# A hybrid decoder layer in float32: gate part moved to the output projection, pinned block products, six open merges

## The chip, the cores and the metric

The kernel runs on one core of one Trainium2 chip. The metric is the device time of one execution in microseconds. The kernel before took 2693.59 us, the median of three runs (2691.98 to 2694.18). All matrix products run on TensorE (PE in the profile); VectorE (DVE) and ScalarE (ACT) prepare operands and take results out of PSUM; GpSimd (POOL) builds some small sums and issues some transfers; SyncE (SP) issues most of the DMA transfers, strictly one after the other.

## The reference, cut to what matters

One layer over 512 tokens of width 2048, one batch. A condition vector `c` gives a shift, a scale and a gate for each channel.

```python
u = RMSNorm(x) * (1 + scale(c)) + shift(c)
# one projection of u (w_in) gives q, k, v of three mixers, their z and the merge gates g
A: differential attention, 8 heads: (softmax(q1 k1) - lam * softmax(q2 k2)) @ v, RMS norm
B: retention, 8 heads, q and k rotated in pairs, decay matrix instead of softmax, RMS norm
C: dilated sliding windows, 3 groups x 8 heads
y_b = (mixer_b(u) * silu(z_b)) @ P_b            # 1024 -> 2048, for b in A, B, C
m   = sum_b sigmoid(g_b) * y_b
x   = x + gate(c) * (m @ W_out)
out = RMSNorm(x) * w
```

The gate is `gate(c) = silu(c) @ w_ada[:, 4096:6144] + b_ada[4096:6144]`, a vector of 2048 channels from a matrix of 2048 x 2048 float32, 16 MB. The rotation pairs channel 2i with 2i+1: `x * cos + swap(x) * sin`, where the swap exchanges the two and changes a sign. All values are float32; the kernel reaches that accuracy by splitting each operand in a high part `h` (rounded to the matmul type) and a low part `l = x - h`, and by three matmuls for each product: h·h, h·l and l·h (`mm3`).

## The kernel before, in words

Channels lie on partitions, 128 at a time, and the 512 tokens along the free dimension. The normalised input is `uh`, `ul` (16 blocks of 128 channels). The program has nine stages in time:

1. Start and forms (0 to 243 us): norms, shift and scale, and the token sides `fh`, `fl` of the block products.
2. Block products (243 to 968): the values of the three mixers and the merge gates of A and B, each a unit of 1024 columns by a scheme of seven products of half-size blocks. A unit is a list of jobs; a job has a preparation (load a raw block `xr`; for the sums, four in-place adds at L583; the cast `xh` on ScalarE, L552 or L584; the low part `xl` on VectorE, L553 or L585) and a multiplication. When a list ends, a closing (`keep`, `p2_done`, `sum_done` at L604 to L614) takes the products out of PSUM and hands the result on: values are stored by GpSimd, gates go through a sigmoid first.
3. C heads (968 to 1665): projections of one head after another, scores, softmax, values. Beside them GpSimd builds one bias a head for the merge gates of C (L674 to L687): four loads of weights, products with the shift, and sums into a tile `br`; TensorE adds its rows up (L691) and VectorE stores the column.
4. Merge of C (1665 to 1760), a call of `gate_phase`: 16 output blocks `db`. Each is a product of eight weight blocks (`w_half`: load of 512 KB, cast at L147, low part at L148) with `yh`, `yl`, the mixer's result in eight row blocks; then VectorE multiplies by the gate column `gsg`, adds the partial sum `gpr` of the earlier mixers, and stores it to `part`, from where the next merge reads it.
5. A heads (1760 to 2090). 6. Merge of A (2090 to 2175).
7. B (2175 to 2410): four pairs of heads, each with two rotations (L1102 to L1106), the splits of `q` and `k` (L1136 to L1146), scores and values. 8. Merge of B (2410 to 2510), whose closing gives the merged operand `mh`, `ml` instead of a partial sum.
9. Output projection (2510 to 2692): five groups of output columns (512, 512, 512, 256, 256). For each step of a group a tile of `w_out` is loaded, cast (L1223), split (L1224) and multiplied with four token blocks; then `residual` multiplies by `gate`, adds `x` (`hx`) and collects squares; the final norm follows.

In a merge, the last row blocks of `y` are not ready when it begins. So `y_start` opens three products with the first six of the eight row blocks, between which leftover work of the mixer stands (`left`), and each product is closed in turn with the last two row blocks. Within the merges of C and A stands the gate part (L768, called by `gate_aux` after each close): 32 pieces of 512 KB of `w_ada` (`gwa`) are loaded on SP, each folded by two VectorE operations into `gacc`; after eight pieces a sum over partitions by two matmuls (`gate_sum`) is added to a row (`grow`) that is stored to DRAM and later loaded, spread over 128 partitions, as `gate` (L1215).

The order on each engine is the order in which a scheduler places the recorded instructions, by its own estimate of when they become ready; a queue runs them strictly in that order, and an instruction that waits holds back those behind it. PSUM has eight banks: two tagged `pj`, six tagged `at`. Weight tiles have three buffers, the raw blocks of the block products three and their split parts two, `gsg` two, `gpr` one, `br` one.

## Time and profile before

| | |
|---|---|
| median of three runs | 2693.59 us |
| time of the profiled execution | 2694.27 us |
| its span from first to last instruction | 2692.5 us |
| mean granted TensorE clock | 0.986 of full |
| TensorE busy | 2578.1 us, 96% |
| VectorE busy | 1695.3 us, 63% |
| ScalarE busy | 1034.6 us, 38% |
| GpSimd busy | 268.9 us, 10% |
| DMA | 448 MB, 166 GB/s on average |

A row of instructions names the line of the program, the engine, the operation, the tile written and the tiles read, their shape, how many there were, the busy time, the mean duration of one in ns, and the engine's idle time in front of them with what ended it. A row of waits gives the line that waited, who released it, the total, the number of waits and the longest. Durations of single matmuls overlap, since TensorE is pipelined; their start-to-start distance is what counts.

### The profile page before, as it was taken

The numbers are of one execution on the slowest core, as the hardware profiler recorded it, in microseconds if no ns is written. First come the engines' busy times: TensorE is split into PE (matmuls) and PEld (weight loads), VectorE is DVE, ScalarE is ACT, GpSimd is POOL, SyncE is SP. The second block draws the span as 40 slices with busy tenths as digits, with TensorE's granted clock in tenths as the row PEclk, the third lists the DMA queues.
The fourth block names the chain that finished last, engine by engine and source line by source line (L and its number), as shares of the span: only waits on it lengthen the run. The fifth ranks groups of instructions, "written<-read, shape, count | busy, mean of one in ns | idle before, by whom it ended". The sixth has DMA issues, their size and how long they took to land.

```text
span 2692.5 us, 33258 instructions
## 1 busy us (share of the span) xinstructions
PE 2578.1 (96%) x13091; PEld 2188.5 (81%) x13091; DVE 1695.3 (63%) x2456; ACT 1034.6 (38%) x1388; POOL 268.9 (10%) x271
## 2 busy tenths in 40 slices
PE   6899999999999999899999999999999899998998
PEld 5677878789999988788888888788887677777888
DVE  7995887877787744334443444657766667776434
ACT  4234433333343433333333333246665134443222
POOL 3432000000000022132211220000000000000000
PEclk9999999999999999999999999999999899999999
DMA  9776666666656655334444444943232773325632
GB/s 347 247 275 239 231 212 219 219 220 209 212 196 204 208 145 137 94 106 126 113 118 108 112 125 128 286 126 87 86 94 84 231 236 90 106 82 176 219 102 102
DMA packets 413420, 448.17 MB, mean 166 GB/s; under 512 B 24696, under 2 KB 308042, under 8 KB 412112
## 3 DMA queue, kind: packets, MB, share of 16 engines
q1 hardware_dynamic: 383784, 395.61, 46.6%
q0 software_dynamic: 9760, 33.59, 4.0%
q10 hardware_dynamic: 19720, 16.86, 1.8%
q8 instruction: 102, 1.67, 0.3%
q14 instruction: 54, 0.44, 0.1%
HBM read 405.56 MB, written 40.44 MB: 166 GB/s over the span
## 4 chain that ended last, share of the span: by engine, by line
PE 78%; DVE 12%; DMA 5%; ACT 2%; issue 2%; POOL 0%; SPq 0%; DVEq 0%; ACTq 0%; POOLq 0%
PE pj L154 15%; PE pj L153 15%; PE pj L152 15%; PE at L154 10%; PE at L153 10%; PE at L152 10%; DVE acc L312 3%; DMA xr<-in_w_in_dram 2%; DVE xl L553 1%; DMA part<-gsg 1%; DVE rt L1105 1%; DVE rs L995 1%; DMA gpr<-part 1%; DVE wl L148 1%; ACT xh L552 1%
## 5 line engine op out<-in xcount | busy, mean ns | idle before, releaser
L154 PE MATMUL pj<-uh,wl 128*128 128x512 f32 x1552 | 610.2, 393 | 12.1 <-DVE wl L148 9.5
L152 PE MATMUL pj<-uh,wh 128*128 128x512 f32 x1552 | 614.1, 396 | 4.8 <-ACT wh L147 4.8
L153 PE MATMUL pj<-ul,wh 128*128 128x512 f32 x1552 | 608.5, 392 | 0.0
L148 DVE TENSOR_TENSOR wl<-wr,wh 128x1024 fp32r<-128x1024 f32 x226 | 282.4, 1251 | 368.0 <-ACT wh L147 349.2
L147 ACT CAST wh<-wr 128x1024 fp32r<-128x1024 f32 x228 | 239.0, 1050 | 540.3 <-PE pj L153 395.3
L154 PEld LDWEIGHTS pj<-uh,wl 128*128 128x128 f32 x1552 | 293.8, 189 | 76.3 <-DVE wl L148 11.9
L152 PEld LDWEIGHTS pj<-uh,wh 128*128 128x128 f32 x1552 | 294.1, 189 | 63.9 <-ACT wh L147 5.0
L153 PEld LDWEIGHTS pj<-ul,wh 128*128 128x128 f32 x1552 | 294.0, 189 | 58.6
L584 ACT CAST xh<-xr 128x2048 fp32r<-128x2048 f32 x72 | 137.6, 1912 | 235.8 <-PE at L154 104.1
L583 DVE TENSOR_TENSOR xr<-xr 128x512 f32<-128x512 f32 x288 | 197.3, 690 | 41.5 <-DMA xr<-in_w_in_dram 36.0
L585 DVE TENSOR_TENSOR xl<-xr,xh 128x2048 fp32r<-128x2048 f32 x72 | 164.7, 2289 | 43.3 <-ACT xh L584 43.1
L152 PE MATMUL at<-yh,wh 128*128 128x512 f32 x384 | 155.2, 405 | 18.4 <-ACT yh L218 11.8
L553 DVE TENSOR_TENSOR xl<-xr,xh 128x2048 fp32r<-128x2048 f32 x54 | 123.8, 2293 | 55.3 <-ACT xh L552 54.8
L154 PE MATMUL at<-yh,wl 128*128 128x512 f32 x384 | 154.5, 402 | 3.9 <-DVE wl L148 3.7
L153 PE MATMUL at<-yl,wh 128*128 128x512 f32 x384 | 153.9, 401 | 0.0
L552 ACT CAST xh<-xr 128x2048 fp32r<-128x2048 f32 x54 | 103.0, 1908 | 128.0 <-PE at L153 52.0
L152 PE MATMUL at<-fh,xh 128*128 128x256 f32 x384 | 108.7, 283 | 0.0
L153 PE MATMUL at<-fl,xh 128*128 128x256 f32 x384 | 108.7, 283 | 0.0
L154 PE MATMUL at<-fh,xl 128*128 128x256 f32 x384 | 108.7, 283 | 0.0
L152 PEld LDWEIGHTS at<-yh,wh 128*128 128x128 f32 x384 | 74.8, 195 | 36.0 <-ACT yh L218 13.0
L153 PE MATMUL at<-xl,fh 128*128 128x512 f32 x240 | 93.5, 390 | 1.1 <-DVE xl L553 1.1
L154 PE MATMUL at<-xh,fl 128*128 128x512 f32 x240 | 93.4, 389 | 0.0
(408 smaller groups left out, 5144.9 us busy)
## 6 DMA issues: line engine op xcount, KB each, us to landing
wr<-in_w_in_dram SPq DMA_DIRECT2D x196, 512.0 KB, 3.9
xr<-in_w_in_dram SPq DMA_DIRECT2D x144, 512.0 KB, 4.4
xr<-in_w_in_dram SPq DMA_DIRECT2D x54, 1024.0 KB, 5.6
wa<-in_w_ada_dram SPq DMA_DIRECT2D x20, 1024.0 KB, 9.8
gwa<-in_w_ada_dram SPq DMA_DIRECT2D x32, 512.0 KB, 5.7
wr<-in_w_out_dram SPq DMA_DIRECT2D x32, 512.0 KB, 3.8
wr<-in_w_in_dram SPq DMA_DIRECT2D x32, 448.0 KB, 6.7
wb<-in_w_ada_dram SPq DMA_DIRECT2D x12, 1024.0 KB, 8.8
```

The costliest lines, as they stand in the source:

```text
L147: act.copy(h, r)
L148: low.tensor_sub(l, r, h.bitcast(F32))
L152: nc.tensor.matmul(ps, lhsT=ah, rhs=bh, start=start, stop=False)
L153: nc.tensor.matmul(ps, lhsT=ah, rhs=bl, start=False, stop=False)
L154: nc.tensor.matmul(ps, lhsT=al, rhs=bh, start=False, stop=stop)
L312: dve.scalar_tensor_tensor(out=acc, in0=wa[:, j, :], scalar=sc[:, k:k + 1], in1=acc, op0=ALU.mult, op1=ALU.add)
L552: act.copy(h, r)
L553: dve.tensor_sub(l, r, h.bitcast(F32))
L583: dve.tensor_add(r[:, o, :], r[:, o, :], r[:, a, :])
L584: act.copy(h, r)
L585: dve.tensor_sub(l, r, h.bitcast(F32))
L995: dve.reciprocal(rs, rs)
```

## The change

Six edits in one:

- **Block products.** The order of their matmuls, casts, splits, sums and sigmoids on the engines is pinned to the order in which they are written (`keep_in_program_order`), and the loop over the jobs is written as three steps: the raw block of two jobs ahead is loaded, the next job's block is summed and split, the present job is multiplied. A unit's closing is cut in three (`done_z`, `done_s`, `done_rest`), one behind each of three following jobs; a gate's sigmoid comes one job later still.
- **Biases.** `br` has two buffers, a load starts in each head and its sum is taken in the next, and the doubled load stands at head 4 instead of head 1.
- **Merges.** In C and A six products are opened with seven of the eight row blocks, in B four with six; one tile (`late`) holds the last row blocks' weights for all of them. The first two products use the `pj` banks. From then on each further product is a whole one, and a close follows each (two in B, while more than one is behind).
- **Gate part.** It moves from the merges of C and A to the output projection: two pieces after each step of the first column group, one after each later step, with two buffers for `gwa`. `gate` is loaded as the bias `b_ada`, spread over the partitions, and the sums are added to it in place; the row `grow` and its way through DRAM are gone.
- **Rotation.** The four VectorE products of 32 rows that read the swapped rows become four ScalarE copies and one VectorE product of 128 rows; the table `sin` is loaded swapped, in four pieces. The second copy of a low part of `k` is made by ScalarE.
- **B's end.** The values of the last pair's first head move into the last projection.

```diff
+    def pin(instr):
+        if pinned[0]:
+            tc.keep_in_program_order(instr)
...
     for i, (_, mul, done) in enumerate(jobs):
-        nxt = jobs[i + 1][0]() if i + 1 < len(jobs) else None
-        if i < HJ:
-            form_build(i)
+        sums = form_build(i) if i < HJ else None
+        due, deferred[:] = list(deferred), []
+        if i + 2 < len(jobs):
+            raws.append(jobs[i + 2][0]())
+        nxt = x_split(raws.pop(0)) if raws else None
+        if sums:
+            form_split(*sums)
+        for f in due:
+            f()
         mul(ready)
         ready = nxt
-        if done is not None:
-            done()
+        later += done
+        for _ in range(len(later) if len(done) == 1 else min(1, len(later))):
+            later.pop(0)()
...
-        br = pool.tile([P, P], F32, tag="br", name="br", bufs=1)
+        br = pool.tile([P, P], F32, tag="br", name="br", bufs=2)
...
-        if hd == 1:
-            bias_step()
+        if hd == 4:
+            bias_more()
...
+        n_ahead, late, places = {"first": (6, 1, (0, 2)), "mid": (6, 1, (0, 1, 2)), "last": (4, 2, (0, 1))}[mode]
...
-        for db in range(3):
-            ahead[db] = y_start(db)
-            if left:
+        for db in range(n_ahead):
+            ahead[db] = y_start(db, 8 - late)
+            if db in places:
                 left.pop(0)()
+        r, h7, l7 = w_tiles([P, late, n_ahead * P])
+        nc.sync.dma_start(out=r, in_=w_p[0, 1024 - late * P:1024, 0:n_ahead * P].rearrange("(j p) c -> p j c", p=P))
...
-            if aux is not None:
-                aux(db)
+        done = 0
+        for db in range(n_ahead, KC):
+            ahead[db] = y_start(db, 8)
+            for _ in range(2 if mode == "last" and db - done > 1 else 1):
+                close(done)
+                done += 1
+        for db in range(done, KC):
+            close(db)
...
-    nc.sync.dma_start(out=sin, in_=k_sin)
+    for to in range(0, P, 32):
+        nc.sync.dma_start(out=sin[to:to + 32, :], in_=k_sin[to ^ 32:(to ^ 32) + 32, :])
...
-        dve.tensor_mul(t1, ps, cos)
         for to in range(0, P, 32):
             at_ = to ^ 32
-            dve.tensor_mul(t2[to:to + 32, :], ps[at_:at_ + 32, :], sin[at_:at_ + 32, :])
+            act.copy(t2[to:to + 32, :], ps[at_:at_ + 32, :])
+        dve.tensor_mul(t1, ps, cos)
+        dve.tensor_mul(t2, t2, sin)
...
-    nc.sync.dma_start(out=gate, in_=gate_dram[0].partition_broadcast(P))
+    nc.sync.dma_start(out=gate, in_=b_ada[0, 2 * D:3 * D].partition_broadcast(P))
...
+            for _ in range(2 if n == 0 else 1):
+                gate_part()
```

The change moves instructions on several engines. Three places follow, rows as the built programs have them (line, operation, tile written and tiles read, shape, and how many stand together).

VectorE, at the closing of a unit of the block products, before: `z`, `s`, `r` are the closing, `xr` the four sums and `xl` the split of a coming job.

```order
L604 TENSOR_TENSOR z<-pj,p_2651 128x512 x2
L553 TENSOR_TENSOR xl<-xr,xh 128x2048
L606 TENSOR_TENSOR s<-z,at 128x512 x2
L610 TENSOR_TENSOR z<-z,at 128x512
L607 TENSOR_TENSOR r_2629<-r_2629,s 128x1024
```

And after:

```order
L610 TENSOR_TENSOR z<-pj,p_2657 128x512 x2
L507 TENSOR_TENSOR xl<-xr,xh 128x2048
L616 TENSOR_TENSOR s<-z,at 128x512 x2
L617 TENSOR_TENSOR r_2635<-r_2635,s 128x1024
L507 TENSOR_TENSOR xl<-xr,xh 128x2048
L623 TENSOR_TENSOR z<-z,at 128x512
```

A second split now stands between the sum `r` and the rest of the closing.

SP, from the load of `gate` in the output projection, before: `wr` is a tile of `w_out`, `hx` a block of `x`.

```order
L1195 DMA wr<-in_w_out_dram 128x2x512
L1215 DMA gate<-gated 128x2048
L1216 DMA finw<-in_final_norm_w_dram 128x2048
L1227 DMA hx_19447<-in_x_dram 128x2048
L1227 DMA hx_19448<-in_x_dram 128x2048
L1195 DMA wr<-in_w_out_dram 128x2x512
L1227 DMA hx_19449<-in_x_dram 128x2048
L1195 DMA wr<-in_w_out_dram 128x2x512 x2
L1227 DMA hx_19450<-in_x_dram 128x2048
L1195 DMA wr<-in_w_out_dram 128x2x512 x16
```

And after:

```order
L1200 DMA wr<-in_w_out_dram 128x2x512 x2
L1258 DMA gate<-in_b_ada_dram 128x2048
L1259 DMA finw<-in_final_norm_w_dram 128x2048
L1232 DMA gwa<-in_w_ada_dram 128x2x512 x2
L1270 DMA hx_19295<-in_x_dram 128x2048
L1232 DMA gwa<-in_w_ada_dram 128x2x512 x2
L1270 DMA hx_19296<-in_x_dram 128x2048
L1232 DMA gwa<-in_w_ada_dram 128x2x512 x2
L1270 DMA hx_19297<-in_x_dram 128x2048
L1232 DMA gwa<-in_w_ada_dram 128x2x512 x2
L1200 DMA wr<-in_w_out_dram 128x2x512 x2
L1232 DMA gwa<-in_w_ada_dram 128x2x512 x2
```

Eight loads of the gate part now stand between the sixth and the seventh tile of `w_out`.

VectorE in the same place, after: `wl` is the split of a tile of `w_out`, `gacc` the gate part's operations, `gl` and `gate` its closing sum. Before, the splits alone stood here, seven in a row.

```order
L1267 TENSOR_TENSOR wl<-wr,wh 128x1024 x2
L1237 TENSOR_SCALAR gacc<-gwa,sc 128x512
L1239 SCALAR_TENSOR_TENSOR gacc<-gwa,sc,gacc 128x512 x3
L1267 TENSOR_TENSOR wl<-wr,wh 128x1024
L1239 SCALAR_TENSOR_TENSOR gacc<-gwa,sc,gacc 128x512 x12
L1245 TENSOR_TENSOR gl<-gacc,gh 128x512
L1267 TENSOR_TENSOR wl<-wr,wh 128x1024
L1220 TENSOR_TENSOR gate<-gate,pj 128x512
L1237 TENSOR_SCALAR gacc<-gwa,sc 128x512
L1267 TENSOR_TENSOR wl<-wr,wh 128x1024
```

The split of the seventh tile stands behind twelve operations of the gate part and the low part of their sum.

247 lines of the change are left out of this document (129 added, 118 removed).

## The prediction

> **What bounds the kernel now.** I read the busy shares of the page first, then the busy time of each engine in nine stretches whose borders are the stages of the program, then who makes TensorE wait, and last the chain of waits and the timeline around the long gaps. The stretches are: start and forms, block products of values and gates, C heads, merge of C, A heads, merge of A, B, merge of B, output projection.
>
> ```profile
> core 0: us, PE busy (x) PEld busy (x) DVE busy (x) ACT busy (x) POOL busy (x), PEclk, DMA share, GB/s
> 0.00:243.00 243.00, 210.56 (x947) 171.85 (x948) 194.50 (x318) 82.63 (x117) 84.06 (x38) 0.98 0.81 279
> 243.00:968.00 725.00, 706.57 (x4352) 635.19 (x4350) 564.95 (x565) 281.81 (x186) 26.87 (x37) 1.00 0.62 211
> 968.00:1665.00 697.00, 685.72 (x3272) 575.50 (x3273) 287.24 (x530) 242.47 (x389) 156.63 (x195) 0.99 0.44 118
> 1665.00:1760.00 95.00, 92.23 (x411) 75.68 (x410) 57.86 (x74) 29.36 (x36) 1.32 (x1) 0.98 0.82 258
> 1760.00:2090.00 330.00, 323.46 (x1509) 267.13 (x1507) 220.72 (x441) 198.10 (x338) 0.00 (x0) 0.99 0.31 92
> 2090.00:2175.00 85.00, 72.47 (x286) 56.78 (x287) 58.50 (x76) 14.43 (x15) 0.00 (x0) 0.92 0.80 258
> 2175.00:2410.00 235.00, 220.65 (x971) 179.33 (x970) 176.40 (x277) 105.36 (x189) 0.00 (x0) 0.98 0.40 117
> 2410.00:2510.00 100.00, 92.16 (x398) 75.20 (x397) 61.58 (x74) 33.16 (x42) 0.00 (x0) 0.95 0.54 163
> 2510.00:2692.00 182.00, 174.24 (x956) 151.82 (x954) 73.56 (x104) 47.27 (x78) 0.00 (x0) 0.99 0.37 135
> ```
>
> The first number after the colon is the length of the stretch, the next TensorE's busy time. TensorE is nearly always busy, so a time can only be saved where it is not. After the start (which the change leaves alone) it is idle for 18.4 + 11.3 + 2.8 + 6.5 + 12.5 + 14.4 + 7.8 + 7.8 = 81.5 us, and the last 7.8 are the tail behind the last matmul, so 74 us can be won from idle time at most. No matmul is removed. The waits behind that idle time:
>
> ```profile
> PE at L152 <- ACT yh L218: 11.8, 3, 6.4
> PE at L691 <- POOL br L686: 10.5, 1, 10.5
> PE pj L154 <- DVE wl L148: 9.5, 6, 1.9
> PE at L152 <- ACT wh L147: 6.6, 2, 6.0
> PE pj L152 <- ACT wh L147: 4.8, 1, 4.8
> PE at L152 <- ACT xh L552: 4.6, 3, 1.5
> PE at L1116 <- ACT k0h L1144: 4.2, 1, 4.2
> PE at L1030 <- DVE e L1021: 3.7, 2, 1.8
> ```
>
> Total, number of waits, longest one. A second loss hangs on the long gaps: the matmuls behind them are slow.
>
> ```profile
> 2107.70 0.39 PE L153 MATMUL at<-yl,wh 128*128 128x512 f32 x1
> ...
> 2112.00 0.39 PE L154 MATMUL at<-yh,wl 128*128 128x512 f32 x1
> ...
> 2122.44 0.80 PE L152 MATMUL at<-yh,wh 128*128 128x512 f32 x1 [5.97 <-ACT wh L147]
> ...
> 2124.75 0.63 PE L153 MATMUL at<-yl,wh 128*128 128x512 f32 x1
> 2125.18 0.63 PE L154 MATMUL at<-yh,wl 128*128 128x512 f32 x1
> ...
> 2128.87 0.39 PE L152 MATMUL at<-yh,wh 128*128 128x512 f32 x1
> ```
>
> Ahead of the gap 19 steps take 4.30 us, 0.227 from start to start; behind it a step is 0.43 (2124.75 to 2125.18). From 2122.44 to 2128.87, where the old pace is back, lie 15 steps, 3.4 us at 0.227, and they took 6.4. So a gap of 6 us costs 9. I count 1 to 3 us of such slow pace for each gap over 4 us. The 0.227 also gives the step used below: 24 matmuls of 512 columns, 5.45 us.
>
> The Trainium skill, page "TensorE: Matmul & The Clock Gate", section "What's actually happening", says that an idle window of about 3.4 us halves the clock and a busy one restores it. By that rule each removed gap returns at most 1.7 us more than itself; this one cost 3.0 more, so the row is used; with 1.7 for each of the five gaps named here the sum would move by a microsecond or two.
>
> **The block products.** The work per step, a row each for the sums and for the split behind them:
>
> ```profile
> L583 DVE TENSOR_TENSOR xr<-xr 128x512 f32<-128x512 f32 x288 | 197.3, 690 | 41.5 <-DMA xr<-in_w_in_dram 36.0
> L585 DVE TENSOR_TENSOR xl<-xr,xh 128x2048 fp32r<-128x2048 f32 x72 | 164.7, 2289 | 43.3 <-ACT xh L584 43.1
> ```
>
> A step that sums costs VectorE 4 × 0.69 + 2.29 = 5.05 us of TensorE's 5.45. Nothing is removed there. What changes is order: raw blocks are loaded two steps ahead (the 36.0 us that L583 waits for its load go), and the closing operations of a unit, eleven of them with hardly a split between, come in three portions between steps. Nine units close; the idle time is 18.4 us, of which some 4 belong to the last closing, where the first C projection waits 4.8 us for its weight split behind the sigmoid of the last portion. That order is unchanged, so it stays. Of the 14 left, one late place per unit remains: the two adds behind P2 (2 × 0.68), four sums (2.76) and a split (2.29) are 6.4 us in one step of 5.45, and the buffers cover a part of it; I leave 0.5 for each of nine. That is **−10** (bounds −15, all of it, and +5: the fixed order lets no ready piece overtake a late one, and 5.05 of 5.45 leaves 0.4 us of slack a step).
>
> **The bias sums in the C heads.** The matmul of L691 waited 10.5 us for a sum that GpSimd built late, since a sum cannot begin before the matmul of the one ahead has read the one buffer:
>
> ```profile
> 1052.54 0.45 POOL L683 TENSOR_TENSOR br<-bw 128x128 f32<-128x128 f32 x1 [37.97 <-PE at L691]
> ```
>
> GpSimd stood idle 38 us in front of it. With two buffers it starts at once, and each sum is taken up a whole head after its load began. GpSimd is busy 157 of 697 us in this stretch, so it has the time. **−11.5**: 10.5 and 1 of slow pace (bounds −12.5 and 0, if the one doubled load at the fifth head comes late in its place).
>
> **Merge of C**: six products open instead of three, the gate parts leave (DMA share was 0.82). 2.8 us of idle time and some slow pace: **−2** (−4 to +4).
>
> **Merge of A.** Before, three products are opened with six of eight row blocks, and then each is closed in turn; the gate parts' loads stand between its loads. Three rows of the stretch's transfers (times to landing) and one of its waits:
>
> ```profile
> gwa<-in_w_ada_dram SPq DMA_DIRECT2D x16, 512.0 KB, 6.2
> gpr<-part SPq DMA_DIRECT2D x14, 256.0 KB, 5.2
> part<-gsg ACTq DMA_DIRECT2D x14, 256.0 KB, 5.0
> PE at L152 <- ACT yh L218: 5.0, 1, 5.0
> ```
>
> Waits that go: 5.0 of L218 (the last row of `yh`, wanted after three products, now after six and a half: 3.5 × 5.45 = 19 us later), 6.0 of L147 (a weight load behind three gate-part loads on SP), 3.7 of L1021 (the transposes now stand inside longer products). Sum 14.7; slow pace behind three of them about 4.5; the matmuls of two gate sums 0.9 (four of 0.227). In all 20.1. Against it: a close is `gpr` landing 5.2, an add of the size of L583's, 0.69, and one buffer, so 5.9 us a close against 5.45 a product; from the ninth product on each waits for a freed bank. Eight products × 0.45 = 3.6 us, less what lower DMA traffic shortens. I take **−18** (−22 to −5, the last if closes need 7 us: 8 × 1.6 = 13 us given back).
>
> **B.** The tables of cosines come ahead of the merge's closes on SP instead of behind them; that removes the 4.2 us on `k0h` and its slow pace (5). The rotation:
>
> ```profile
> L1105 DVE TENSOR_TENSOR rt<-pj,sin 32x512 f32<-32x512 f32 x32 | 22.0, 687 | 0.5
> L1102 DVE TENSOR_TENSOR rf<-pj,cos 128x512 f32<-128x512 f32 x8 | 5.5, 688 | 10.5 <-PE pj L154 6.7 <-DMA cos<-in_k_cos_dram 3.8
> L1144 ACT CAST k1h<-rf 64x512 fp32r<-64x512 f32 x8 | 4.9, 617 | 0.2
> ```
>
> Four products of 32 rows (2.75 us) become four ScalarE copies and one product of 128 rows (0.69): VectorE 4.1 us to 2.1 for each of 8 rotations, and 8 operations on `k` fewer (64 rows, at the same 0.69), 22 us of its 176. ScalarE gains 40 copies of which no row shows a 32-row one; the 64-row copy is 0.62, so 25 us at most on its 105 of 235. The chain of one rotation is no shorter: 4 × 0.62 + 0.69 + 0.69 = 3.9 against 4.1. So only the six waits on L148 (9.5 us, the split behind a busy VectorE) profit; as weight casts now stand behind the copies on ScalarE, I take 4 of the 9.5. **−9** (−14 to 0).
>
> **Merge of B**: 6.4 of the 11.8 on L218 and its pace go, the values come earlier: **−9** (−11 to −3).
>
> **The output projection** takes in what left the merges: 32 loads of 512 KB, 64 VectorE operations, 8 matmuls, 4 adds. The stage has nothing to hide behind on TensorE; there is no idle time between its matmuls (the idle time of a row is its last number). Rows of the stage's TensorE and VectorE work, of the gate part's operations before, and of the transfers from 2505 to 2692:
>
> ```profile
> L153 PE MATMUL at<-wl,mh 128*128 128x512 f32 (+1 forms) x255 | 92.4, 362 | 0.0
> L1224 DVE TENSOR_TENSOR wl<-wr,wh 128x1024 fp32r<-128x1024 f32 x26 | 31.9, 1225 | 72.4 <-ACT wh L1223 72.4
> L782 DVE SCALAR_TENSOR_TENSOR gacc<-gwa,sc,gacc x60: 731/751/754, 1681.4 to 2173.5; 128x512 f32<-128x512 f32 x60
> wr<-in_w_out_dram SPq DMA_DIRECT2D x28, 512.0 KB, 3.7
> hx<-in_x_dram SPq DMA_DIRECT2D x4, 1024.0 KB, 12.5
> GB/s 175 423 426 403 372 172 112 114 112 78 66 85 112 112 112 112 88 56 84 112 112 107 120 102 51 184 302 223 41 0 0 4 0 0 0 118 156 178 224 224
> ```
>
> VectorE's time is there: 64 × 0.75 = 48 us on top of 73.6 of 182. The loads are the risk. In the first column group two gate parts follow each of eight steps, and on SP the weight tiles of steps 6 and 7 stand behind the eighth part's load, with two buffers for parts. Counted from the first matmul of the stage: `gate`, `finw` and the first loads of `x`, 1 MB each, keep the DMA engines full (423 and 426 GB/s in slices of 4.7 us) until about 13 us, so the first two parts land at 13.4. Their four operations end at 16.4. Then each of the two buffers turns over in some 4 us of landing (the weight tiles here take 3.7), 1.5 of its own operations and 0.5 of the other's: 6 for a pair. The fourth pair ends at 16.4 + 18 = 34.4, the closing split of the sum and the split of step 6 at 36.5, wanted at 6 × 5.45 = 32.7: 4 us late. Further on two weight tiles stand behind two pairs at a time: 12 us of parts against 10.9 of steps, and the tile behind them lands, is cast and split late by its own 1.7 more: 3 us late, two or three times until the group's eight steps are through. Later groups take one part a step, 4 + 1.5 against 5.45, no wait. 4 + 3 × 2.7 = **+12** (bounds +4, the first wait alone, and +30: a landing of 6.2 as in the merge of A makes a pair 8.2 and the sixth step 10 late, then four waits of 5).
>
> The sum: −10 − 11.5 − 2 − 18 − 9 − 9 + 12 = −47.5. The profiled execution took 2694.27 us, 1.8 us of it around its span of 2692.5, and stands 0.7 above the median of 2693.59. 2694.3 − 47.5 − 0.7 = **2646 us**.
>
> **Rivals.**
> *The output projection turns bound by its loads, and the kernel becomes slower.* If no weight tile overlaps a pair of parts, a step of the first group takes 6.2 (landing) + 3.0 (four operations) + 3.7 (weight tile) + 2 × 1.23 (cast and split, both at the split's price) = 15.4 us against 5.45, eight times: +79 in place of +12, so 2646 + 67 = 2713. It decides from a loss of 65 upward, a mean step of 13.6 us. For it: SP issues in order, and a waiting part's load blocks the tile behind it. Against it: two tiles are issued together and three buffers let them run ahead. Chance 0.09.
>
> By the Trainium skill ("DMA: Bandwidth & Descriptors", "Where 436 GB/s comes from") a core draws some 358 GB/s from HBM; the first group's 18 MB would then take 50 us of 43.6, or +7. The slices of 423 and 426 GB/s speak against the limit, and +7 is inside my bounds.
>
> *The closes bound the merges.* Closes at 7 us in A give back 13, trail into B and keep its loads late (5), and gain nothing in C and 4 in B's merge: 2646 + 13 + 5 + 2 + 5 = 2671. For it: `gpr` has one buffer and `part` lands in 5.0. Against: the DMA share of 0.80 in that stretch came for more than a third from gate parts (16 × 0.52 of 85 us × 258 GB/s = 21.9 MB). Chance 0.17.
>
> *The fixed order brings nothing*, or holds back: the closings were already between the steps in the recorded order, and the sums' 5.05 of 5.45 leaves the late places where they are. 2646 + 10 = 2656, and 2661 with the outer bound. Chance 0.14.
>
> *Everything fits*: output +4, A −22, B −14, block products −15: 2646 − 8 − 4 − 5 − 5 = 2624. Chance 0.18.
>
> **How the numbers follow.** The forecast, 2646 give or take 12, has 0.42. The range from 2612 to 2682 leaves out the slow case and the outer edges of the others. A difference of 0.2%, 5.4 us, is about what a measurement of this kernel can tell from none. Faster: 0.42 + 0.17 + 0.14 + 0.18 less a few hundredths in which two of the unfavourable cases come together, 0.87; slower 0.09; within 0.2%, 0.04.
>
> **What would show it.** Right, if in the profile after no wait on `br` over 2 us is left, the longest wait on `yh` in the merges is under 2, the `k0h` wait is gone, VectorE in B is near 154 busy us, and the first 45 us of the output projection show TensorE idle in front of a split (L1267) two to four times, 12 us in all. Wrong, if the block products still take 725 us, if products in the merges wait for the add of a close (L779), or if the output stage has idle time behind its first group.

## The result, and the profile after

The changed kernel takes 2664.49 us, the median of four runs (2660.30 to 2669.42), against 2693.89 us (2691.98 to 2697.72) before in the same comparison: a ratio of 0.989 with a 95% interval of 0.9869 to 0.9910. It is faster by 29 us where 47.5 were forecast; 2664.49 lies within the predicted range, some 18 us above the predicted 2646. The profiled execution took 2663.64 us, its span is 2661.9, 30.6 less than before, and the mean granted clock 0.989. One of all the executions in this document, of the kernel with the gate part in the A heads and two buffers, took 4265.14 us at a granted clock of 0.558, and is left out of that kernel's median.

Here are the stretches of the changed kernel behind the start, cut near its own stage borders (length; busy time and count of PE, PEld, DVE, ACT and POOL; granted clock; DMA share; GB/s):

```profile
238.60:961.00 722.40, 711.62 (x4367) 640.31 (x4367) 572.33 (x567) 281.15 (x186) 25.37 (x35) 0.99 0.64 214
961.00:1642.80 681.80, 676.55 (x3244) 567.98 (x3242) 291.33 (x531) 241.23 (x387) 158.20 (x196) 0.99 0.45 120
1642.80:1736.00 93.20, 91.35 (x420) 75.73 (x421) 34.58 (x40) 29.77 (x36) 1.85 (x2) 1.00 0.56 168
1736.00:2047.00 311.00, 308.24 (x1444) 255.33 (x1443) 213.74 (x420) 189.58 (x323) 0.00 (x0) 1.00 0.33 97
2047.00:2144.00 97.00, 93.00 (x409) 75.83 (x408) 46.73 (x67) 28.52 (x40) 0.00 (x0) 0.98 0.57 168
2144.00:2364.00 220.00, 206.30 (x923) 169.20 (x922) 152.28 (x243) 125.72 (x225) 0.00 (x0) 0.98 0.42 122
2364.00:2458.50 94.50, 91.64 (x400) 74.81 (x399) 63.12 (x75) 32.74 (x42) 0.00 (x0) 0.98 0.56 171
2458.50:2661.90 203.40, 183.96 (x970) 157.16 (x968) 123.83 (x178) 50.38 (x83) 0.00 (x0) 0.96 0.61 208
```

Three things are to be seen. The C heads (second row) and the merges of A and B (fifth and seventh) hold TensorE nearly all the time now. B (2144 to 2364) still has 13.7 us without a matmul, although VectorE's busy time in it fell to 152.28. And the output projection, in which before nothing waited until the tail, has become the stretch with the lowest clock, 0.96, and with 19.4 us of idle time, of which 8.3 are the tail behind the last matmul.

To compare stages to the microsecond, each is taken between matmuls, in the same way in every kernel: C heads, A heads, B and the merge of B end with the first matmul of the next stage, the merges of C and A and the output projection with their own last one. The block products end with the last product that reads a token form; the twelve products behind it, and the wait of 4.8 us in front of the first C projection, count to the C heads (6.5 us in both kernels).

| stage | before | after | change | predicted |
|---|---|---|---|---|
| start and forms | 239.1 | 238.6 | −0.5 | 0 |
| block products | 723.1 | 721.1 | −2.0 | −10 |
| C heads | 695.9 | 683.0 | −12.9 | −11.5 |
| merge of C | 96.8 | 93.3 | −3.5 | −2 |
| A heads | 311.5 | 310.9 | −0.6 | 0 |
| merge of A | 116.8 | 96.7 | −20.1 | −18 |
| B | 222.4 | 220.5 | −1.9 | −9 |
| merge of B | 103.0 | 94.4 | −8.6 | −9 |
| output projection | 175.3 | 194.8 | +19.5 | +12 |

The sum is −30.6, the difference of the spans. Four terms came out about as forecast. Three did not: the block products, B and the output projection are 8, 7.1 and 7.5 us worse; the other stages gave 5.7 more than forecast, so 16.9 of the 47.5 are missing. The waits of TensorE after, from the same view as before:

```profile
PE at L158 <- DVE gsg L777: 5.0, 3, 2.3
...
PE pj L1217 <- ACT gh L1244: 4.8, 1, 4.8
...
PE pj L159 <- DVE xl L507: 4.7, 2, 2.8
PE pj L160 <- DVE wl L144: 4.6, 2, 3.3
...
PE at L159 <- DVE xl L507: 4.0, 3, 1.8
PE at L158 <- DVE res L1252: 3.8, 1, 3.8
...
PE at L1119 <- ACT k0h L1147: 2.9, 1, 2.9
...
PE at L158 <- ACT wh L1266: 2.4, 1, 2.4
PE pj L158 <- ACT wh L143: 2.3, 1, 2.3
PE pj L158 <- ACT yh L224: 2.2, 1, 2.2
```

The 10.5 us for `br` are gone, so are the six waits for a split behind the rotation, and the waits for `yh` shrank from 11.8 us to 2.2. New are three in the output projection: the sum of a gate part (L1217), the residual of a column group (L1252) and a weight cast (L1266). L144 and L143 are weight tiles of B, at its start, and both rows for `xl` belong to the block products. The first row is new as well: three times a product of a merge (once in C, 1.9 us, twice in A, 3.1 us) waits for its PSUM bank until VectorE has multiplied a finished product by the gate column (L777), in the close.

### The profile page after: what moved, and what is told of

Same layout as the page of the kernel before. It is cut to its first block, busy times and chain, and to the rows that moved or that the text cites. A ratio compares the mean times of both kernels' runs of the same rounds, so it can differ in the third digit from the quotient of the medians.

```text
span 2661.9 us, 33296 instructions
## 1 busy us (share of the span) xinstructions
PE 2568.5 (96%) x13091; PEld 2184.6 (82%) x13091; DVE 1689.0 (63%) x2427; ACT 1058.6 (40%) x1431; POOL 269.6 (10%) x271
## 4 chain that ended last, share of the span: by engine, by line
PE 74%; DVE 11%; DMA 8%; ACT 3%; issue 2%; SPq 0%; POOL 0%; ACTq 0%; DVEq 0%
PE pj L158 15%; PE pj L160 15%; PE pj L159 15%; PE at L159 8%; PE at L160 8%; PE at L158 8%; DVE acc L318 3%; DMA gpr<-part 2%; DMA gwa<-in_w_ada_dram 1%; DVE xl L507 1%; DMA gsg<-g 1%; DMA xr<-in_w_in_dram 1%; DMA part<-gsg 1%; DMA xr<-ud 1%; DVE xr L592 1%
## 5 line engine op out<-in xcount | busy, mean ns | idle before, releaser
L158 PE MATMUL at<-yh,wh 128*128 128x512 f32 x336 | 131.8, 392 | 5.9 <-DVE gsg L777 5.0
L159 PE MATMUL at<-yl,wh 128*128 128x512 f32 x336 | 131.5, 391 | 0.0
L160 PE MATMUL at<-yh,wl 128*128 128x512 f32 x336 | 131.5, 391 | 0.0
L158 PE MATMUL at<-wh,mh 128*128 128x512 f32 (+1 forms) x256 | 93.1, 369 | 6.2 <-DVE res L1252 3.8
L159 PE MATMUL at<-wl,mh 128*128 128x512 f32 (+1 forms) x256 | 94.9, 371 | 0.2
L160 PE MATMUL at<-wh,ml 128*128 128x512 f32 (+1 forms) x256 | 94.5, 369 | 0.0
L278 POOL TENSOR_TENSOR wl<-wr,wh 128x896 fp32r<-128x896 f32 x32 | 77.3, 2421 | 136.5 <-ACT wh L277 127.3
```

What stands on the lines that cost most here:

```text
L158: pin(nc.tensor.matmul(ps, lhsT=ah, rhs=bh, start=start, stop=False))
L159: pin(nc.tensor.matmul(ps, lhsT=ah, rhs=bl, start=False, stop=False))
L160: pin(nc.tensor.matmul(ps, lhsT=al, rhs=bh, start=False, stop=stop))
L278: nc.gpsimd.tensor_sub(l, r, h.bitcast(F32))
```

## The experiments

All comparisons are with the kernel before on the same chip; "after" is the changed kernel. The stage times come from one profiled execution each. Stages whose code is the same in two kernels mostly agree within 1 or 2 us there, but the block products vary from 717 to 722, B from 218 to 222 and the output projection from 194.8 to 197.4, so a few microseconds in these can't be told.

### The output projection: the gate part left out, and its loads moved

The first kernel leaves the whole gate part out of the output projection; `gate` is then only its bias, which leaves out a part of the computation, and the time is read as that of the other five edits.

```diff
-            for _ in range(2 if n == 0 else 1):
-                gate_part()
```

> The changed kernel with the gate part left out of the output projection (no loads of the gate matrix, no sums; the gate is the bias alone, so the output is not the reference's). In the changed kernel the output projection runs 194.8 us from its first to its last matmul, before it ran 175.3. Theory: the whole difference is the gate part's late sums and late weight tiles and the slow pace behind these gaps. Then the stage falls to 175 to 176 us and the kernel to 2645 (2643 to 2648). Rival: a part of the stage's idle time belongs to the residuals that stand between groups and would be late anyway, so that the stage stays above 180 and the kernel at 2650 or more.

Measured: 2644.95 us (2643.63 to 2646.22), ratio 0.9814 (0.9798 to 0.9830). The output stage is back to 175.3 us, the value of before, and no wait of TensorE is left in it. So the gate part costs 19.5 us where it was moved to, the whole difference of that stage; the theory's number came out.

What the 19.5 are made of is seen in the changed kernel. The first gap in TensorE's timeline, and VectorE's work around the third:

```profile
2490.99 0.39 PE L160 MATMUL at<-wh,ml 128*128 128x512 f32 x1
2496.20 0.79 PE L1217 MATMUL pj<-gh,ones_r 128*128 128x512 f32 x1 [4.82 <-ACT gh L1244]
```

```profile
2558.72 1.22 DVE L1267 TENSOR_TENSOR wl<-wr,wh 128x1024 fp32r<-128x1024 f32 x1
2561.62 1.54 DVE L1239 SCALAR_TENSOR_TENSOR gacc<-gwa,sc,gacc 128x512 f32<-128x512 f32 x2 [1.69 <-DMA gwa<-in_w_ada_dram]
2563.08 1.28 DVE L1252 TENSOR_TENSOR res<-at,gate 128x512 f32<-128x512 f32 x2
```

In the first, TensorE stands in front of the matmul that sums the first eight parts, from 32.6 to 37.6 us into the stage. The products behind it could not have run either: their tile of `w_out` was issued on SP at 2489.84, behind loads of the gate part, and landed at 2495.2, and its cast and its split follow right behind those of the sum:

```profile
2496.06 1.99 ACT L1266 CAST wh<-wr 128x1024 fp32r<-128x1024 f32 x2
2497.13 1.23 DVE L1267 TENSOR_TENSOR wl<-wr,wh 128x1024 fp32r<-128x1024 f32 x1 [0.26 <-ACT wh L1266]
```

In the second, the residual of a column group, which empties the PSUM bank that the next group's first product needs, stands on VectorE behind two operations of the gate part; these wait 1.69 us for their load, and TensorE waits 3.8 us for the residual. With 2.4 us for a cast (L1266) the three waits make 11.0. The eight added matmuls are 1.8 (8 × 0.227). The other 6.7 are mostly slow pace: at or just behind the end of each of the three waits the granted clock is 0.50 for 3.4 us (2496.1 to 2499.5, 2513.2 to 2516.6, 2564.4 to 2567.8), which loses 1.7 us each time, 5.1 in all. The last 1.6 are not accounted for. One row of the stage's transfers:

```profile
wr<-in_w_out_dram SPq DMA_DIRECT2D x28, 512.0 KB, 4.6
```

A weight tile takes 4.6 us to land where it took 3.7. The second kernel moves the loads that nobody needs early (`gate`, `finw`, `x`) behind the parts, spreads the parts over three column groups, and puts each sum where its parts are through.

```diff
+    PARTS = ((2, 2, 2, 2, 0, 0, 1, 1), (1, 1, 1, 1, 1, 1, 0, 0), (2,) * 8, (0,) * 4)
+    SUM_AT = (6, 7, 5, 1)
...
+            if n == 0 and t == 3:  # load gate, finw
+            if n == 0 and t >= 4:  # load hx[t - 4]
+            if t == SUM_AT[n]: gate_sum()
```

> The changed kernel with another order of loads in the output projection: the gate part's first eight pieces come ahead of the loads of gate, finw and x (6 MB), which come in steps 4 to 8; in the first group only ten pieces instead of sixteen, six in the second, two a step in the third; each sum two or three steps behind its last piece. Bytes and operations are the same. Theory: the stalls of the output projection (5.0 us at the seventh step, 2.6 at the ninth, 3.9 at the third group's start, and slow pace behind each) come from the order in which the loads stand on one queue. Then the stage goes from 194.8 to 178 to 184 us and the kernel to 2648 to 2654. Rival: the bytes in the first two groups or VectorE's own order are the limit: the stalls only move, 2660 to 2668.

Measured: 2657.35 us (2657.11 to 2662.31), ratio 0.9864 (0.9850 to 0.9879); output stage 190.3. Its waits:

```profile
PE at L158 <- DVE res L1252: 2.7, 1, 2.7
...
PE pj L1219 <- ACT gh L1244: 1.4, 1, 1.4
```

The sum's wait fell from 4.8 to 1.4 us and the residual's from 3.8 to 2.7; waits for weight tiles (3.9 in all) stand where 2.4 stood. 4.5 us of 19.5 came back in the stage; the result lies between the theory and the rival. A better order alone does not hide the gate part here. The scheduler also put the loads of `gate`, `finw` and the first block of `x` between the first eight parts after all, so the order that was meant was not quite the one that ran.

### The block products: no pin, and a later pin

```diff
     def pin(instr):
-        if pinned[0]:
-            tc.keep_in_program_order(instr)
+        return
```

> The changed kernel with no instruction pinned; the order in which it is written, the closings in three pieces and the loads two jobs ahead stay, the scheduler places the instructions again. The block products took 721 us in the changed kernel and 723 before. Theory: the fixed order is what made the closings nearly free (0.26 us of idle time at each of three unit borders, 1.70 before) and it costs nothing elsewhere. Then without it the borders cost 1 to 2 us each again, the stage is 4 to 8 us longer and the kernel at 2669 to 2673. Rival: the pieces and the earlier loads do it, and the fixed order holds back the first eight jobs, where 10 us of idle time and 6 us of slow pace stand between 240 and 380. Then the stage is shorter by up to 8 and the kernel at 2657 to 2664.

Measured: 2662.85 us (2661.17 to 2663.75), ratio 0.9880 (0.9865 to 0.9894); block products 717.6. Without the pin the time is the same as with it, and the theory that the pin was worth several microseconds falls. Why is seen when the stage is cut in three. First before, then after, then the kernel without the pin:

```profile
239.10:320.00 80.90, 77.29 (x331) 62.84 (x330) 67.90 (x82) 37.20 (x30) 2.19 (x3) 0.98 0.73 257
320.00:400.00 80.00, 76.81 (x336) 62.66 (x335) 65.98 (x68) 27.66 (x16) 2.69 (x4) 1.00 0.62 210
400.00:962.20 562.20, 554.59 (x3691) 511.36 (x3690) 428.51 (x416) 214.90 (x139) 20.49 (x28) 1.00 0.61 207
```

```profile
238.60:320.00 81.40, 75.61 (x313) 60.45 (x313) 67.31 (x80) 37.46 (x30) 2.19 (x3) 0.96 0.70 249
320.00:400.00 80.00, 76.02 (x326) 61.89 (x325) 66.03 (x68) 27.76 (x16) 2.69 (x4) 0.98 0.61 207
400.00:959.70 559.70, 558.69 (x3720) 516.67 (x3719) 437.70 (x419) 215.93 (x140) 20.49 (x28) 1.00 0.63 210
```

```profile
238.60:320.00 81.40, 77.95 (x329) 63.30 (x328) 67.17 (x82) 37.40 (x30) 2.19 (x3) 0.96 0.73 258
320.00:400.00 80.00, 79.67 (x349) 64.78 (x348) 68.09 (x71) 28.10 (x17) 2.69 (x4) 1.00 0.63 211
400.00:956.40 556.40, 551.38 (x3683) 509.96 (x3682) 426.87 (x413) 214.16 (x139) 20.50 (x28) 1.00 0.63 209
```

The first number in brackets is the count of matmuls. From 400 us on the pin does what was forecast of it: 1.0 us without a matmul, against 7.6 before and 5.0 without the pin. Up to 400 us it does the reverse: 639 matmuls, against 667 before and 678 without the pin. 28 matmuls fewer than before are 6.4 us at 0.227. So from before to after the late part gains about what the early one loses, and the stage gains 2 us instead of 10. Against the kernel without the pin, which differs in nothing else, the pin saves 4.0 us late and loses 39 matmuls, 8.9 us, early.

The early part is where the token forms are built beside the products, and VectorE is busy for 83% of it. One place where the fixed order holds up there is ScalarE at 358 us after: a copy of finished products waits for a store to free its tile, and the next block's cast stands behind it; without the pin the same copy waits for its matmuls alone.

```profile
358.78 1.07 ACT L574 COPY r<-pj 128x512 f32<-128x512 f32 x2 [3.95 <-DMA vd<-r]
```

```diff
-    pinned[0] = True
     for i, (_, mul, done) in enumerate(jobs):
+        pinned[0] = i >= HJ
```

> The changed kernel with the order pinned only from the ninth job on. Pinned from the start the block products take 721.1 us, unpinned 717.6; in the first 140 us the pinned order has 10 us of idle time (splits that wait for loads behind the form rows, which share the raw blocks' three buffers), the unpinned one 4; later the unpinned one has 6 us more at the unit borders. Theory: the two effects are separate. Then this one has both advantages, 713 to 716: the kernel at 2656 to 2660. Rival: the early gaps belong to the loads, not to the order, and stay: 2662 to 2666.

Measured: 2661.45 us (2658.92 to 2663.81), ratio 0.9878 (0.9863 to 0.9892); block products 719.0. Three microseconds below after, with overlapping ranges. Up to 400 us this kernel does 652 matmuls; the 13 that it has more than after all lie before 320 us, while the stretch from 320 to 400 stays as slow as with the full pin. So the loss is not one of the forms' order alone, and by time the run is inconclusive. That the pin causes the early loss is shown by the counts in all fourteen profiles: from 320 to 400 us the eleven kernels that are pinned there have 326 to 333 matmuls, the two without the pin (this section's first and the last kernel of this document) 349 and 350.

### B: the rotation before, and a second buffer for the partial sums

```diff
+        dve.tensor_mul(t1, ps, cos)
         for to in range(0, P, 32):
-            act.copy(t2[to:to + 32, :], ps[at_:at_ + 32, :])
-        dve.tensor_mul(t2, t2, sin)
+            dve.tensor_mul(t2[to:to + 32, :], ps[at_:at_ + 32, :], sin[at_:at_ + 32, :])
...  # both low parts of k by VectorE, sin loaded unswapped
```

> The changed kernel with the rotation and the low parts of k as before: four products of 32 rows on VectorE, no copies on ScalarE. The B stage took 220.5 us in the changed kernel, of which some 2 belong to values moved in from the merge, and 222.5 before. Theory: the rotation on ScalarE is worth the six waits for weight splits that were there before (9.5 us) and are gone now, so that undoing it costs 7 to 12 us: the kernel at 2672 to 2677, with waits of L154's kind on wl back in every pair. Rival: it is worth what I predicted, 4 us: 2668. Second rival: what the copies save on VectorE they take on ScalarE, 2664 as now.

Measured: 2677.11 us (2675.97 to 2678.50), ratio 0.9934 (0.9919 to 0.9948), 12.6 us more than after; B 231.9 instead of 220.5. The six waits behind the rotation are back, as is the busy row that it stands for:

```profile
PE pj L160 <- DVE wl L147: 9.7, 6, 2.1
```

```profile
L1106 DVE TENSOR_TENSOR rt<-pj,sin 32x512 f32<-32x512 f32 x32 | 22.0, 687 | 0.6
```

So the rotation, together with the copy of the low part of `k`, is worth 11 to 12.6 us, all of the 9.5 us of waits and their slow pace, where the prediction took 4. In its place after:

```profile
L1106 ACT COPY rt<-pj x32: 575/578/583, 2169.7 to 2339.5; 32x512 f32<-32x512 f32 x32
L1108 DVE TENSOR_TENSOR rt<-rt,sin x8: 678/681/682, 2174.8 to 2341.3; 128x512 f32<-128x512 f32 x8
```

ScalarE, which had the time, does the 32 copies in 0.578 us each. If the rotation gave 11, though, then B lost 9 elsewhere, since it is only 1.9 shorter; some 2 of these are the values that moved in from the merge. The rest is lost at its start:

```profile
2144.00:2190.00 46.00, 36.13 (x140) 28.51 (x139) 26.00 (x42) 19.80 (x35) 0.00 (x0) 0.89 0.65 193
```

10 us idle in 46, at a granted clock of 0.89. The queues point to a cause. ScalarE's waits in the first 28 us of B, a piece of its timeline, and VectorE's adds of the closes of this merge:

```profile
ACT wh L143 <- DVE gsg L779: 4.9, 1, 4.9
ACT wh L146 <- DVE gsg L779: 4.1, 1, 4.1
```

```profile
2146.84 0.33 ACTq L781 DMA_DIRECT2D part<-gsg  x1
2147.27 1.38 ACT L143 CAST wh<-wr 128x256 fp32r<-128x256 f32 x4 [4.88 <-DVE gsg L779]
```

```profile
L779 DVE TENSOR_TENSOR gsg<-gsg,gpr x16: 684/691/694, 2087.1 to 2173.6; 128x512 f32<-128x512 f32 x16
...
  DMA gpr<-part: 19.8, 10
```

The closes of the merge of A trail into B. Each stores its result by an issue on ScalarE's queue (L781), which has to wait for VectorE's add (L779), and VectorE waits for `gpr`, 10 times, 19.8 us in all. The weight casts of B (L143) stand behind these issues on ScalarE. A second buffer for `gpr` is to test that:

```diff
-                pr = gp.tile([P, S], F32, tag="gpr", name="gpr", bufs=1)
+                pr = (qp if mode == "mid" and db % 2 else gp).tile([P, S], F32, tag="gpr", name="gpr", bufs=1)
...  # cos, sin, dec in a pool of their own; B's pool opened with reuse_waits="tile"
```

> The changed kernel with a second buffer for the partial sums (gpr) in the merge of A; the three tables of B get a pool of their own, so that they are still loaded early. In the changed kernel the last closes of A's merge run until 2174, 30 us into the B stage, each waiting for its partial sum to land (5 to 6 us a close), and the first B projections stand idle 1.5, 2.5, 3.5 and 3.1 us behind weight splits and the first rotation, which stand behind these closes on VectorE and behind their stores on ScalarE's queue; slow pace behind it makes some 14 us. Theory: the single buffer sets the rate of the closes; with two they keep up with the products and end within a few us of them. Then 8 to 13 us go: the kernel at 2652 to 2657. Rival: the two gate-column buffers, which wait for the store of a close, set the same rate: 2661 to 2665.

Measured: 2663.36 us (2658.83 to 2665.89), ratio 0.9883 (0.9868 to 0.9898). In the profile B is 212.3, 8 us shorter, and the merge of A 98.3, 1.6 longer; the median over the runs is 1 us below that of after. By time that is no difference. The run also changed the pool of B's tiles, and no run has the buffer without the new pool, so the 8 us of the profile can't be put down to the buffer alone.

What the profiles say of the closes (times from the merge's first product to the start of a close's add; "trail" is how long after B's first matmul the last add starts; the last three kernels come further below):

| kernel | first close | last close | mean spacing | trail | B |
|---|---|---|---|---|---|
| before (old rotation) | 32.3 | 125.7 | 6.23 | 8.1 | 222.4 |
| after | 40.1 | 126.6 | 5.77 | 29.6 | 220.5 |
| two buffers for `gpr`, new pool | 40.1 | 115.3 | 5.02 | 16.8 | 212.3 |
| three open products | 30.0 | 113.6 | 5.58 | 17.4 | 219.4 |
| gate part in A, two buffers, new pool | 41.1 | 116.7 | 5.04 | 19.5 | 216.5 |
| gate part in A, three open products | 29.1 | 111.4 | 5.49 | 15.5 | 216.1 |
| all three (the last kernel below) | 29.1 | 103.7 | 4.97 | 7.1 | 206.6 |

Six open products delay the first close by 10 us; one buffer lets a close through every 5.8 us against 5.45 for a product, so the last one is done no earlier than before, while the products end 20 us sooner. B does not follow the trail alone: with three open products the trail is as short as with two buffers, and B is hardly shorter than in after.

### The merges: three open products instead of six

```diff
-        n_ahead, late, places = {"first": (6, 1, (0, 2)), "mid": (6, 1, (0, 1, 2)), "last": (4, 2, (0, 1))}[mode]
+        n_ahead, late, places = {"first": (3, 2, (0, 2)), "mid": (3, 2, (0, 1, 2)), "last": (3, 2, (0, 1))}[mode]
```

> The changed kernel with three products opened in each merge, six of eight row blocks in each, as before, instead of six, six and four; the gate part stays in the output projection. The merge of A took 116.9 us before from its first to its last product and 96.7 in the changed kernel. Theory: the larger part of these 20 us is the gate part's absence (loads on the queue, 6.0 of wait and its pace, sums); the six open products give the 5.0 us wait on the last row of y, the 3.7 of the transposes and their pace. Then A's merge takes 104 to 108 and B's 3 to 7 more: the kernel at 2675 to 2682. Rival: with the loads gone the last row comes in time anyway: 2665 to 2669.

Measured: 2658.89 us (2656.80 to 2662.78), ratio 0.9869 (0.9852 to 0.9885). The theory expected this to be slower, by 10 us or more; it is not, it is if anything 5 us faster, and in the merge of A the rival's reason, that the last row comes in time anyway, holds. The merge of A takes 96.0 us (96.7 with six), that of C 91.0 (93.3). The largest row of waits in the merge of A, with three and with six (the others are under 1 us):

```profile
PE at L160 <- DVE wl L147: 2.8, 1, 2.8
...
```

```profile
PE at L158 <- DVE gsg L777: 3.1, 2, 2.3
...
```

Neither has the wait of 5.0 for `yh` that stood there before. In this kernel too, a whole product, the fourth, stands between the opened ones and the first close. So the 20 us of the merge of A are not bought by six open products. What both kernels share, and the kernel before lacks, is that the gate part's loads are gone from the merge, the order of a whole product ahead of each close, and the use of the two `pj` banks. Which of these gives how much was not separated.

### The biases with one buffer

```diff
-        br = pool.tile([P, P], F32, tag="br", name="br", bufs=2)
+        br = pool.tile([P, P], F32, tag="br", name="br", bufs=1)
```

> The changed kernel with one buffer for the bias sums (br), their loads in the same places. Theory: the next sum waits again until TensorE has read the one ahead; the wait on br comes back, 10 us or more in all with its slow pace: the kernel at 2673 to 2685. Rival: the place of the doubled load (fifth head instead of second) alone did it: 2664.

Measured, two runs: 2677.61 us (2676.07 to 2679.15), ratio 0.9938 (0.9918 to 0.9958), 13 us more than after. C heads 695.3, and the wait is back to the tenth:

```profile
PE at L724 <- POOL br L719: 10.5, 1, 10.5
```

The whole 12.9 us of the stage hang on the second buffer; the earlier loads of the biases give nothing without it. Whether the buffer would do it without the earlier loads was not run.

### The gate part beside the heads of A, and what the other findings add

If the gate part fits neither in the merges nor in the output projection, the A heads are a place: DMA share 0.33 there, VectorE busy 214 of 311 us. The next kernel loads it in 64 pieces of 256 KB, eight a head, sums them into a row, and stores that row for the output projection to load as `gate`.

```diff
+        if gsum:
+            gate_sum()
+        for _ in range(3):
+            gate_part()
         ps = proj(A_K + hd * P, mid=left[1])
...
+        for _ in range(3):  # behind K; two more behind Z
+            gate_part()
...
-            for _ in range(2 if n == 0 else 1):
-                gate_part()
```

> The changed kernel with the gate part moved once more, from the output projection to the A heads (64 pieces of 256 KB, eight a head, two buffers; the four sums go to DRAM as a row and come back as gate). There the DMA share is 0.3 and VectorE is busy 220 of 330 us. Without the gate part the kernel took 2645 and with it in the output projection 2664.5. Theory: in the A heads its 48 us of VectorE and 16 MB lie beside TensorE's work, only the 8 matmuls (1.8 us) and a few waits are added. Then the output projection is back at 175 and the kernel at 2646 to 2652. Rival: VectorE's order lets pieces that wait for their load stand ahead of the softmax and the splits of A, and the A heads get 10 us or more longer: 2656 to 2665.

Measured: 2657.14 us (2651.97 to 2659.24), ratio 0.9863 (0.9846 to 0.9879). The output stage is back to 175.3, but the A heads went from 310.9 to 322.2:

```profile
PE at L1013 <- DVE k1l L1108: 7.4, 8, 2.6
PE pj L158 <- DVE sz L207: 2.9, 1, 2.9
```

Eight times the scores wait for a low part of `k` (2.8 us in all in after); in three of the eight heads, with 4.4 of the 7.4 us, it stands on VectorE right behind two gate operations. Of the 19.5 us, 11 are paid again: VectorE had free time in the stage, but not at those places.

```diff
+                pr = (qp if mode == "mid" and db % 2 else gp).tile(...)   # to the kernel with the gate part in A
```

> The kernel of the run before with a second buffer for the partial sums in the merge of A as in the run e5_two_partials. There the B stage was 8 us shorter in the profile (212 against 220), but the medians showed 1 us, with 7 us between single runs. Theory: the closes that trail into B cost 8 us and the spread of the output projection hid it; with the gate part gone from there the difference shows: 6 to 10 us faster than the run before it in this call. Rival: the gain is given back elsewhere: within 2 us of it.

Measured: 2654.05 us (2651.61 to 2656.60, three runs), ratio 0.9849 (0.9832 to 0.9865): 3 us below the one before it, with overlapping ranges. The second buffer alone is again not shown to help.

```diff
+        n_ahead, late, places = {"first": (3, 2, (0, 2)), "mid": (3, 2, (0, 1, 2)), "last": (3, 2, (0, 1))}[mode]
```

> The kernel with the gate part in the A heads, and three products opened in each merge instead of six, six and four. In the run e6_three_open this was not slower than the changed kernel, 2658.9 against 2664.5. Theory: the number of open products is worth nothing once the gate part is out of the merges; the difference to the run e9_gate_in_a is within 3 us, or some us in favour of three. Rival: e6 gained by chance of the spread, six are worth 3 us or more.

Measured: 2646.78 us (2644.20 to 2648.54), ratio 0.9821 (0.9806 to 0.9836). 10 us below the kernel with six open products, and the ranges don't touch: with the gate part in A, three are better than six.

The last kernel has the gate part in A, the second buffer, three open products, and no pin.

> The kernel with the gate part in the A heads, two buffers for the partial sums, three open products and nothing pinned. If the effects add up: e10_gate_in_a_two_partials, less 2 for the merge of C, and the same for the pin: 2636 to 2644. If two of them touch the same wait (trailing closes start later with three open products): 2644 to 2650.

Measured: 2639.87 us (2639.19 to 2641.35), ratio 0.9797 (0.9782 to 0.9812): 54 us faster than before and 25 faster than after, the fastest of all. The closes trail by 7.1 us (last row of the table above), and the first 46 us of B, which answer to 2144 to 2190 in after, are:

```profile
2152.60:2198.60 46.00, 45.43 (x204) 37.18 (x203) 29.40 (x56) 25.58 (x49) 0.00 (x0) 1.00 0.55 162
```

TensorE is busy 45.43 of 46 us at a clock of 1.00, where it was busy 36.13 in after, and the first matmul of B's scores starts 28.7 us after B's first matmul instead of 41.3. B as a whole takes 206.6 against 220.5 us. The kernel with the gate part in A and two buffers has the same buffers and pools as this one, and differs in the six open products and in the pin of an earlier stage: its closes trail by 19.5 us and its B takes 216.5. So some 10 us of B go with the later trail. What the buffer, the new pool and the open products each give was not separated.

## Why the prediction was right or wrong, point by point

- **Biases** (−11.5; measured −12.9, and 13 when undone): right, cause and size. No wait on `br` is left.
- **Merge of A** (−18; −20.1) and **merge of C** (−2; −3.5): the sizes are right, and the three waits named did go. One reason was wrong: I put the vanished wait for `yh` down to six open products, and it vanishes with three as well. The wait for a freed bank that I charged with 3.6 us in A came as two waits of 3.1 on L777, the multiplication just ahead of the add (L779) that I had named as a sign of being wrong. The longest wait on `yh` in the merges is 2.2, a little over the 2 that I had set.
- **Merge of B** (−9; −8.6): right in size, but some 2 us of it are matmuls that the edit moved into B.
- **B** (−9; −1.9): two terms failed in opposite directions. The rotation was taken at 4 of the 9.5 us of its waits; it gave 11 to 12.6, and no wait of that kind is left behind ScalarE's copies. VectorE's busy time came out at 152, as forecast (154). Against that stands what I had as the rival "the closes bound the merges": closes that trail into B. I priced that at 5 and tied it to closes of 7 us, with a chance of 0.17; it happened with closes of 5.8 us, beside the forecast, and cost some 7 to 9. That the two errors nearly cancel in the length of B is luck. What I got wrong is the end of the sum: I compared 5.9 us a close with 5.45 a product and charged 3.6 us in the merge, but did not ask where the last close would end when the products in front end 20 us sooner and the closes start 10 us later. The wait on `k0h` did not go, it fell from 4.2 to 2.9.
- **Block products** (−10; −2, and by time the same without the pin): the step that failed is that the order costs nothing. I summed the idle time of the whole stage. From 400 us on the forecast held, 7.6 us of idle time became 1.0; in the 160 us before, which my sum does not treat apart, the fixed order lost what that brought. The bound of +5 named the reason, "lets no ready piece overtake a late one". The rival "the fixed order brings nothing" had 0.14 and holds for the stage as a whole.
- **Output projection** (+12; +19.5): the mechanism was right for the first wait, which was found almost to the place: from 32.6 to 37.6 us into the stage, where I had 32.7 to 36.5, for a tile that SP issued behind the parts; only the matmul that waits is the sum's, not one behind the split. Of the two or three further waits of 3 us in the first group one came, 2.4 us, at the start of the second. "Later groups … no wait" was wrong: the residual of a group waits behind a gate operation whose load has not landed, 3.8 us. That the waits add up to 11.0, near my 12, is in part luck. Missing from my sum were the 1.8 us of the eight matmuls and the slow pace, most of 6.7 us, which I had counted in the terms of the biases, the merges and B.

The slow pace matters in several of these terms. Behind a gap of 2.4 us in the merge of A after, the matmuls run so:

```profile
2093.77 0.39 PE L160 MATMUL at<-yh,wl 128*128 128x512 f32 x1
2096.43 0.49 PE L158 MATMUL at<-yh,wh 128*128 128x512 f32 x1 [2.28 <-DVE gsg L777]
...
2098.43 0.63 PE L160 MATMUL at<-yh,wl 128*128 128x512 f32 x1
2098.86 0.63 PE L158 MATMUL at<-yh,wh 128*128 128x512 f32 x1
...
2100.38 0.39 PE L159 MATMUL at<-yl,wh 128*128 128x512 f32 x1
```

From 2096.43 to 2100.38 are ten steps, 2.3 us at 0.227, and they took 3.95: 1.7 us on top of 2.4. The granted clock is 0.50 from 2096.74 to 2100.16. The prediction counted slow pace for gaps over 4 us only. By the Trainium skill, page "TensorE: Matmul & The Clock Gate", section "What's actually happening", the clock halves after an idle window of about 3.4 us. This gap is shorter and the clock behind it is halved all the same, so the measurement decides against reading that as a threshold for a gap.

## What to carry to other kernels

A transfer chain that is off the critical path (load, add, store with one buffer) must be followed to where its last link ends once the work in front of it gets shorter; here it ran 30 us into the next stage, and that stage's casts stood behind its issues on a shared queue. Work that is moved to a stage with free engine time pays for the places at which it stands, not for its time: the same gate part cost 19.5 us in one stage and 11 in another, though VectorE had idle time in both. Undo each edit alone before crediting it: here the pin was worth nothing, the six open products cost 10 us once the gate part stood in A, and the rotation gave nearly three times what was thought.

## What the runs showed of the hardware that was not expected

- A gap of 2.4 us on TensorE was followed by 3.4 us at a granted clock of 0.50 (steps of 0.43 instead of 0.227), 1.7 us on top of the gap. In all fourteen traces the slow stretches lie on a grid of windows of 3.41 us, and each fills one, two or three of them. Counted from 250 us on: where TensorE was idle for 2.0 us or more of a window at full clock, the next window was slow in 91 of 91 cases; below 1.4 us in 0 of 9502; between the two in 24 of 69. So in these traces what counts is how much idle time falls into one window, not the length of a gap.
- The number of rows hardly matters for a VectorE product or a ScalarE copy out of PSUM. Before, a product takes 0.687 us for 32 rows by 512 (L1105) and 0.688 for 128 rows (L1102); after, a copy takes 0.578 us for 32 rows by 512 (L1106) and 0.588 for 128 rows (L574). So a job over four quarters costs four whole operations on either engine.
